# Two network blocks on one core: a weight unit split by full-width instructions, hi products ahead of lo products

## The chip, the cores and the metric

The kernel runs on one core of a Trainium2 chip. The time is the device's time of one execution in microseconds, the median of three runs. The engines are TensorE (PE; its weight loads are PEld), VectorE (DVE), ScalarE (ACT), GpSimd (POOL) and SyncE (SP), which issues the loads.

## What is computed

256 tokens with 1024 channels go through two network blocks in float32. The reference, cut to its frame (the helpers are told in words behind it):

```python
def first_block(x, ...):
    h = rmsnorm(x, norm1_g)
    a_val, a_gate, q, k, v, f_logit, g_a, g_b = jnp.split(h @ w_in, idx, axis=-1)
    ya = conformer_conv(a_val, a_gate, conv_w, conv_b, conv_ln_g, conv_ln_b, w_conv_out)
    ob = forgetting_attention(heads(q), heads(k), heads(v), c)
    yb = ob.transpose(0, 2, 1, 3).reshape(B, S, FOX_W) @ w_fox_out
    x = x + (jax.nn.sigmoid(g_a) * ya + jax.nn.sigmoid(g_b) * yb) @ w_out
    x = x + peer_ffn(rmsnorm(x, norm2_g), peer_wq, peer_k1, peer_k2, peer_u, peer_v)
    return rmsnorm(x, normf_g)

def second_block(x, mem, ...):
    z = rms_norm(x, norm_mix[l]) @ w_in[l]
    ...
    x = x + jnp.sum(gates * proj, axis=2) @ w_out[l]
    up = causal_dwconv(rms_norm(x, norm_ffn[l]) @ w_up[l], ffn_conv_w[l], ffn_conv_b[l])
    gate_h, val_h = jnp.split(up, 2, axis=-1)
    x = x + (jax.nn.gelu(gate_h, approximate=True) * val_h) @ w_down[l]
    return rms_norm(x, final_norm[l])
```

The first block has a causal convolution of 31 taps, an attention with 16 heads and a layer of 16384 experts (two products with 16384 x 1024 weights, and a top-16 choice out of 128 x 128 keys). The second has a recurrent branch, a gated linear attention and an attention over a memory, then a feed-forward layer of width 3072.

## The kernel before

All weights are float32 in DRAM and are used once. They come in *units* of 128 x 1024 (some narrower): `load` (lines 226 to 229) brings a unit into one of three `raw` buffers, and `unit` (231 to 252) splits it exactly into two parts of the type float32r: `hi` is the rounded copy, made by ScalarE (line 240), and `lo` is the rest, `raw - hi`, by VectorE (lines 248, 250) or for a share of the halves by GpSimd (line 244). The split goes by halves of 512 columns. `hi` and `lo` have four tiles of 512 columns each (`WBUFS`), which is two units. A tile is free for a later unit when the last product that reads it is done.

The other operand, the activations with their channels on the partitions, is split in the same way into `xh` and `xl`. A product is the sum of hi·xh, hi·xl and lo·xh.

- `ws` (254 to 265) has the weights as the stationary operand: 24 products of 256 columns for one unit. It goes half by half: eight with hi, four with lo, and again.
- `ts_step` and `ts_part` (267 to 277) have the activations as the stationary operand and the weights moving: 12 products of 512 columns for one unit, which accumulate into four banks `accs[t][n]` (t: half of the tokens, n: half of the unit). For each t the order is xh·hi, xh·lo, xl·hi.
- `ts_tail` (279 to 285) takes the last two units of such a sum together, bank by bank, so that the first tokens' sums end early.

The stages in their order, by the profiled execution: the input norm and the convolution's inputs, w_v, and q, k and the gates with the attention (to some 210 us); the output products of the first block; a norm (near 308); the first product of the experts, with the top-k choice and the scatter of the gates beside it (to some 790); the second product of the experts (ts, to 1144); the second block's norm and branches (to 1462); a norm (near 1464); and the feed-forward.

Several things set the order of the work. A scheduler orders each engine's instructions, and `tc.high_priority` moves a unit's load and split ahead of other work. Each engine then works through its list strictly in that order. Under the convolution, 20 of the 31 taps of a channel tile are VectorE's (`conv_tap`, line 394), each reading what the one before it wrote; the other taps are products by ScalarE (line 400) that GpSimd adds up (line 401). `conv` (423 to 431) queues the taps behind the latest split with `tc.issue_after(last_lo[0])`. In `norm_T` (362 to 375) the residual is added (line 318), squared and summed by ScalarE (319), a reciprocal root taken (324, 325), the rows scaled (370), transposed by TensorE (358) and split with the gain (331 on ScalarE, 332 on VectorE). `behind` makes the subtractions of the next unit wait for the scaling.

Of the kernel before, what the change touches and what calls it, by code (L numbers as in the profile page):

```python
# [19 lines left out]
P = 128  # L20
# [6 lines left out]
WBUFS = 4  # L27
# [20 lines left out]
# columns of the packed per-channel vectors  # L48
# [24 lines left out]
def layout(inp):  # L73
# [37 lines left out]
    # a tile of 128: a head's 96 channels and a third of the last head's  # L111
# [54 lines left out]
def tile_kernel(ctx: ExitStack, tc: tile.TileContext, A: dict, out: bass.AP, tap=None):  # L166
# [54 lines left out]
    pri = [0]  # L221
    last_lo = [None]
    behind = [0, None]  # so many splits wait for that instruction
# [7 lines left out]
    def unit(ap, n):  # L231
        """[128, n] from DRAM -> two halves [128, n/2], each as (hi, lo)"""
        out = []
        with tc.high_priority(offset=pri[0]):
            raw = load(ap, n)
            for c in (0, n // 2):
                hi = stream.tile([P, 512], F32R, name="whi", bufs=WBUFS)
                lo = stream.tile([P, 512], F32R, name="wlo", bufs=WBUFS)
                src, hi, lo = raw[:, c:c + n // 2], hi[:, :n // 2], lo[:, :n // 2]
                act.copy(hi, src)  # L240
                shift[1] += shift[0]
                if shift[1] >= 1:  # a share of them for GpSimd
                    shift[1] -= 1
                    gp.tensor_sub(lo, src, hi.bitcast(F32))  # L244
                elif behind[0] > 0:
                    behind[0] -= 1
                    with tc.issue_after(behind[1]):
                        last_lo[0] = dve.tensor_sub(lo, src, hi.bitcast(F32)).ins
                else:
                    last_lo[0] = dve.tensor_sub(lo, src, hi.bitcast(F32)).ins  # L250
                out.append((hi, lo))
        return out

    def ws(o, ap, width, xt, kc=8):
        """o[n, t] = sum_k w[k, n] x[k, t]"""
# [3 lines left out]
        for i, (hi, lo) in enumerate(w):  # L259
            c = [slice(k * width, (k + 1) * width) for k in range(hk)]  # L260
            for k in range(hk):
                pe.matmul(o, hi[:, c[k]], xh[:, i * hk + k, :], start=(i + k == 0), stop=False)  # L262
                pe.matmul(o, hi[:, c[k]], xl[:, i * hk + k, :], start=False, stop=False)  # L263
            for k in range(hk):
                pe.matmul(o, lo[:, c[k]], xh[:, i * hk + k, :], start=False, stop=(i == 1 and k == hk - 1))  # L265

    def ts_part(accs, w, xh, xl, t, first, last, ns=(0, 1)):
# [5 lines left out]
    def ts_step(accs, ap, width, xh, xl, first, last):  # L273
        """accs[t][n] += x[k, t] w[k, n] for one k; xh, xl: [128, 256]"""
        w = unit(ap, width)
        for t in range(2):
            ts_part(accs, w, xh, xl, t, first, last)
# [1131 lines left out]
```

## Time and profile before

| | |
|---|---|
| median of three runs | 1680.26 us (1679.18, 1680.26, 1681.85) |
| span of the profiled execution | 1679.7 us |
| TensorE busy | 1636.7 us (97%), 11346 products |
| VectorE busy | 1239.0 us (74%) |
| ScalarE busy | 1059.9 us (63%) |
| GpSimd busy | 263.1 us (16%) |
| mean granted clock of TensorE | 0.997 |

The page gives the profiled execution's time as its span, from the first to the last instruction; a timed run also has what lies around it. A share over the whole span mixes stages: under the convolution VectorE has no gaps, in the experts' second product it has many. Products overlap, so that a busy TensorE may still stand still for short times; the distance from one product's start to the next tells more. An instruction's duration is longer than its distance to the next one on the same engine, as the next begins before it has quite ended.

### The profile page before, as it was taken

The page shows a single profiled execution, that of the slowest core. Times are in us where ns is not written, and L with a number is a line of the kernel's source. Part 1 is how long each engine was busy: PE and PEld are TensorE (multiplying, and loading weights), DVE is VectorE, ACT ScalarE, POOL GpSimd, SP SyncE. Part 2 cuts the span into 40 slices and gives each one's busy share as a digit, 9 for nine tenths or more (in the row PEclk, how much of TensorE's full clock was granted, in tenths as well). Part 3 has the DMA queues.
Part 4 walks back from the last instruction along what each step waited for, and adds up shares of the span by engine and source line. Part 5 has one row for each costly group of instructions (what it writes and reads, how often), then busy time and mean ns, then how long its engine had stood idle before and what let it go on. Part 6 is the DMA issues. An engine that isn't in the chain of part 4 may idle for free.

```text
span 1679.7 us, 31312 instructions
## 1 busy us (share of the span) xinstructions
PE 1636.7 (97%) x11346; PEld 1525.6 (91%) x11346; DVE 1239.0 (74%) x2616; ACT 1059.9 (63%) x2337; POOL 263.1 (16%) x255
## 2 busy tenths in 40 slices
PE   7899999999999999999999999999999999999998
PEld 7788999899999999999888888888999999899997
DVE  7999967677989997666656665557765556787777
ACT  7767675555567778776555555556776555566665
POOL 5434200000015444443000000001310000000000
PEclk9999999999999999999999999999999999999999
DMA  5443355555654444445666666666444355565553
GB/s 170 140 151 103 124 154 182 172 176 184 180 180 148 134 139 152 150 142 184 190 192 190 194 188 191 198 191 201 158 136 152 102 183 178 177 201 186 184 184 136
DMA packets 79963, 280.49 MB, mean 167 GB/s; under 512 B 9008, under 2 KB 10304, under 8 KB 79808
## 3 DMA queue, kind: packets, MB, share of 16 engines
q1 hardware_dynamic: 79520, 277.96, 52.6%
q8 instruction: 89, 1.46, 0.4%
q14 instruction: 66, 0.54, 0.1%
q10 hardware_dynamic: 288, 0.52, 0.1%
HBM read 277.40 MB, written 1.05 MB: 166 GB/s over the span
## 4 chain that ended last, share of the span: by engine, by line
PE 84%; DVE 9%; ACT 2%; issue 2%; DMA 1%; POOL 1%; SPq 0%; POOLq 0%; DVEq 0%; ACTq 0%
PE acc L270 30%; PE mm L265 16%; PE mm L262 16%; PE mm L263 16%; DVE wlo L250 3%; PE acc L835 3%; DVE ca L394 2%; ACT whi L240 1%; PE mm L1026 1%; DMA raw<-in_w_mk_dram 0%; PE mm L733 0%; DMA raw<-in_w_conv_in_dram 0%; DVE oh L780 0%; DVE oh L777 0%; POOL cg L401 0%
## 5 line engine op out<-in xcount | busy, mean ns | idle before, releaser
L250 DVE TENSOR_TENSOR wlo<-raw,whi 128x512 fp32r<-128x512 f32 (+2 forms) x987 | 661.0, 691 | 278.3 <-ACT whi L240 272.8
L240 ACT CAST whi<-raw 128x512 fp32r<-128x512 f32 (+1 forms) x1060 | 620.3, 606 | 358.9 <-PE mm L263 220.5
L262 PE MATMUL mm<-xT_hi,whi 128*128 128x256 f32 (+1 forms) x2024 | 514.9, 287 | 3.2 <-ACT sgA L579 1.1
L263 PE MATMUL mm<-xT_lo,whi 128*128 128x256 f32 (+1 forms) x2024 | 507.1, 283 | 0.0
L262 PEld LDWEIGHTS mm<-xT_hi,whi 128*128 128x128 f32 (+1 forms) x2024 | 386.5, 191 | 6.5 <-DVE xT_lo L332 1.9
L263 PEld LDWEIGHTS mm<-xT_lo,whi 128*128 128x128 f32 (+1 forms) x2024 | 387.0, 192 | 1.1
L265 PE MATMUL mm<-xT_hi,wlo 128*128 128x256 f32 (+1 forms) x2024 | 327.6, 284 | 9.7 <-DVE wlo L250 9.5
L265 PEld LDWEIGHTS mm<-xT_hi,wlo 128*128 128x128 f32 (+1 forms) x2024 | 278.8, 191 | 13.6 <-DVE wlo L250 13.1
L270 PE MATMUL acc<-whi,ah 128*128 128x512 f32 x512 | 158.6, 390 | 0.0
L270 PE MATMUL acc<-whi,al 128*128 128x512 f32 x512 | 158.2, 389 | 0.0
L270 PE MATMUL acc<-wlo,ah 128*128 128x512 f32 x512 | 158.2, 389 | 0.0
L244 POOL TENSOR_TENSOR wlo<-raw,whi 128x512 fp32r<-128x512 f32 x69 | 96.7, 1401 | 378.3 <-ACT whi L240 299.3
L325 POOL TENSOR_TENSOR rs<-rs,mhalf 128x1 f32<-128x1 f32 x14 | 10.1, 720 | 784.5 <-DVE rs L324 784.5
L270 PEld LDWEIGHTS acc<-wlo,ah 128*128 128x128 f32 x512 | 96.1, 188 | 20.2 <-DVE wlo L250 0.2
L270 PEld LDWEIGHTS acc<-whi,al 128*128 128x128 f32 x512 | 96.1, 188 | 20.0
L270 PEld LDWEIGHTS acc<-whi,ah 128*128 128x128 f32 x512 | 95.7, 188 | 19.8 <-ACT whi L240 0.2
L299 DVE TENSOR_TENSOR al<-S,ah 128x512 fp32r<-128x512 f32 x64 | 44.2, 692 | 70.0 <-ACT ah L298 70.0
L394 DVE SCALAR_TENSOR_TENSOR ca<-zc,pk,ca 128x256 f32<-128x256 f32 x152 | 91.3, 603 | 1.7
L298 ACT CAST ah<-S 128x512 fp32r<-128x512 f32 x64 | 39.8, 623 | 78.7 <-PE acc L270 78.7
L262 PE MATMUL mm<-h_hi,whi 128*128 128x256 f32 (+1 forms) x344 | 88.1, 288 | 0.0
L263 PE MATMUL mm<-h_lo,whi 128*128 128x256 f32 (+1 forms) x344 | 86.7, 284 | 0.0
L401 POOL TENSOR_TENSOR cg<-cg,cm 128x256 f32<-128x256 f32 x80 | 73.9, 925 | 21.2 <-ACT cg L397 8.3
(436 smaller groups left out, 2414.5 us busy)
## 6 DMA issues: line engine op xcount, KB each, us to landing
raw<-in_u_dram SPq DMA_DIRECT2D x128, 512.0 KB, 3.6
raw<-in_v_dram SPq DMA_DIRECT2D x128, 512.0 KB, 3.6
raw<-in_w_up_dram SPq DMA_DIRECT2D x48, 512.0 KB, 3.7
raw<-in_z_gate_dram SPq DMA_DIRECT2D x24, 512.0 KB, 3.8
raw<-in_w_down_dram SPq DMA_DIRECT2D x24, 512.0 KB, 4.1
raw<-in_w_br_dram SPq DMA_DIRECT2D x24, 384.0 KB, 2.9
raw<-in_w_conv_in_dram SPq DMA_DIRECT2D x16, 512.0 KB, 3.6
raw<-in_w_out_dram SPq DMA_DIRECT2D x16, 512.0 KB, 3.8
```

Of the source, the lines that this page charges most:

```text
L240: act.copy(hi, src)
L244: gp.tensor_sub(lo, src, hi.bitcast(F32))
L250: last_lo[0] = dve.tensor_sub(lo, src, hi.bitcast(F32)).ins
L262: pe.matmul(o, hi[:, c[k]], xh[:, i * hk + k, :], start=(i + k == 0), stop=False)
L263: pe.matmul(o, hi[:, c[k]], xl[:, i * hk + k, :], start=False, stop=False)
L265: pe.matmul(o, lo[:, c[k]], xh[:, i * hk + k, :], start=False, stop=(i == 1 and k == hk - 1))
L270: pe.matmul(accs[t][n], l[:, t * P:(t + 1) * P], w[n][p], start=(first and f), stop=(last and e))
L298: act.copy(hi, src)
L299: dve.tensor_sub(lo, src, hi.bitcast(F32))
L394: dve.scalar_tensor_tensor(ca[:, cb, :], z, w, ca[:, cb, :], op0=OP.mult, op1=OP.add)
L401: gp.tensor_add(cg[cb], cg[cb], m)
L835: pe.matmul(b[:, i, :], o1[:, i, :], o2[:, i, :], start=True, stop=True)
```

## The change

`unit` takes one `hi` and one `lo` tile of 1024 columns, of which there are now two each, so the memory is the same. One copy and one subtraction make them. Where GpSimd has its share, it takes the first half of `lo` and VectorE the rest. `behind` counts units and not halves. In `ws` all 16 hi products of a unit come before its 8 lo products; in `ts_step` all 8 hi products, for both halves of the tokens, come before the 4 lo products. In `ts_part` the order is xh·hi, xl·hi, xh·lo, in the tail too. Which products are formed, and from what, is as before.

```diff
-WBUFS = 4
+WBUFS = 2
...
             raw = load(ap, n)
-            for c in (0, n // 2):
-                hi = stream.tile([P, 512], F32R, name="whi", bufs=WBUFS)
-                lo = stream.tile([P, 512], F32R, name="wlo", bufs=WBUFS)
-                src, hi, lo = raw[:, c:c + n // 2], hi[:, :n // 2], lo[:, :n // 2]
-                act.copy(hi, src)
-                shift[1] += shift[0]
...
+            hi = stream.tile([P, 1024], F32R, name="whi", bufs=WBUFS)
+            lo = stream.tile([P, 1024], F32R, name="wlo", bufs=WBUFS)
+            act.copy(hi[:, :n], raw[:, :n])
+            shift[1] += 2 * shift[0]
+            c = 0
+            if shift[1] >= 1:
+                shift[1] -= 1
+                c = n // 2
+                gp.tensor_sub(lo[:, :c], raw[:, :c], hi[:, :c].bitcast(F32))
+            with tc.issue_after(behind[1]) if behind[0] > 0 else nullcontext():
+                last_lo[0] = dve.tensor_sub(lo[:, c:n], raw[:, c:n], hi[:, c:n].bitcast(F32)).ins
+            behind[0] = max(0, behind[0] - 1)
+        return [(hi[:, c:c + n // 2], lo[:, c:c + n // 2]) for c in (0, n // 2)]
...
-        for i, (hi, lo) in enumerate(w):
-            c = [slice(k * width, (k + 1) * width) for k in range(hk)]
+        c = [slice(k * width, (k + 1) * width) for k in range(hk)]
+        for i, (hi, _) in enumerate(w):
             for k in range(hk):
                 pe.matmul(o, hi[:, c[k]], xh[:, i * hk + k, :], start=(i + k == 0), stop=False)
                 pe.matmul(o, hi[:, c[k]], xl[:, i * hk + k, :], start=False, stop=False)
+        for i, (_, lo) in enumerate(w):
             for k in range(hk):
                 pe.matmul(o, lo[:, c[k]], xh[:, i * hk + k, :], start=False, stop=(i == 1 and k == hk - 1))
...
-        for (l, p, f, e) in ((xh, 0, True, False), (xh, 1, False, False), (xl, 0, False, True)):
+        for (l, p, f, e) in ((xh, 0, True, False), (xl, 0, False, False), (xh, 1, False, True)):
+            if "hl"[p] not in parts:
+                continue
...
-        for t in range(2):
-            ts_part(accs, w, xh, xl, t, first, last)
+        for part in "hl":
+            for t in range(2):
+                ts_part(accs, w, xh, xl, t, first, last, parts=part)
...
-                behind[:] = [2, i.ins]
+                behind[:] = [1, i.ins]
```

How the instructions stand, at two places. VectorE under the convolution's inputs (`wlo` is a lo tile, `ca` the sum of the taps, `zc` their input), before:

```order
L250 TENSOR_TENSOR wlo_657<-raw_654,whi_656 128x512
L394 SCALAR_TENSOR_TENSOR ca_161<-zc_159,pk_74,ca_161 128x256
L250 TENSOR_TENSOR wlo_661<-raw_654,whi_660 128x512
L394 SCALAR_TENSOR_TENSOR ca_161<-zc_159,pk_74,ca_161 128x256 x2
L250 TENSOR_TENSOR wlo_694<-raw_691,whi_693 128x512
L394 SCALAR_TENSOR_TENSOR ca_161<-zc_159,pk_74,ca_161 128x256
L250 TENSOR_TENSOR wlo_698<-raw_691,whi_697 128x512
```

The same place in the changed program:

```order
L245 TENSOR_TENSOR wlo_609<-raw_606,whi_608 128x1024
L393 SCALAR_TENSOR_TENSOR ca_161<-zc_159,pk_74,ca_161 128x256 x3
L245 TENSOR_TENSOR wlo_642<-raw_639,whi_641 128x1024
L442 TENSOR_TENSOR zc_159<-mm_502,sg_602 128x256
L393 SCALAR_TENSOR_TENSOR ca_161<-zc_159,pk_74,ca_161 128x256 x3
```

The three taps of a unit, which the second half's subtraction parted, now follow each other.

ScalarE at the norm ahead of the feed-forward (`hrow0`, `hrow1` are the squares of the two halves of the tokens, `whi` the copies of the next two units), before:

```order
L319 ACTIVATE hrow0_17906,ss_17908<-x0_67 128x512
L240 CAST whi_17979<-raw_17977 128x512
L319 ACTIVATE hrow0_17906,ss_17908<-x0_67 128x512
L240 CAST whi_17983<-raw_17977 128x512
L319 ACTIVATE hrow1_17907,ss_17916<-x1_68 128x512
L240 CAST whi_18018<-raw_18016 128x512
L319 ACTIVATE hrow1_17907,ss_17916<-x1_68 128x512
L240 CAST whi_18022<-raw_18016 128x512
L331 ACTIVATE xT_hi_17928<-mm_17930,gcol_69 128x256
```

The same place in the changed program:

```order
L318 ACTIVATE hrow0_16143,ss_16145<-x0_67 128x512 x2
L237 CAST whi_16216<-raw_16214 128x1024
L318 ACTIVATE hrow1_16144,ss_16153<-x1_68 128x512
L237 CAST whi_16251<-raw_16249 128x1024
L318 ACTIVATE hrow1_16144,ss_16153<-x1_68 128x512
L330 ACTIVATE xT_hi_16165<-mm_16167,gcol_69 128x256
```

Two whole copies stand now before the last two squares, where single halves stood between all of them.

## Rows read from the trace of the kernel before

**Rows 1.** Busy time by stretch: us, then busy us of each engine (instructions), clock, DMA

```profile
24.00:94.00 70.00, 59.78 (x385) 51.45 (x384) 68.43 (x107) 49.55 (x106) 38.16 (x41) 0.98 0.44 137
...
108.00:180.00 72.00, 65.45 (x493) 61.70 (x493) 71.22 (x163) 47.80 (x127) 31.97 (x35) 0.98 0.37 115
...
798.00:1134.00 336.00, 336.00 (x1491) 278.28 (x1490) 201.79 (x326) 178.36 (x328) 0.56 (x1) 1.00 0.61 192
...
1344.00:1428.00 84.00, 84.00 (x704) 84.00 (x703) 51.72 (x97) 47.38 (x90) 0.00 (x0) 1.00 0.55 180
```

**Rows 2.** Waits of TensorE, whole span, then 1134 to 1260: us, times, longest us

```profile
PE mm L265 <- DVE wlo L250: 9.8, 14, 2.1
...
PE acc L270 <- DVE wlo L250: 3.2, 4, 1.2
...
PE mm L265 <- DVE wlo L250: 1.6, 3, 0.7
```

**Rows 3.** Groups by form: xcount, busy us, mean ns; of 24-94, 108-180, 798-1134, whole span

```profile
L250 DVE TENSOR_TENSOR wlo<-raw,whi 128x512 fp32r<-128x512 f32 x36 | 31.5, 892 | 0.7 <-ACT whi L240 0.7
...
L250 DVE TENSOR_TENSOR wlo<-raw,whi 128x512 fp32r<-128x512 f32 x31 | 25.8, 834 | 0.1
...
L250 DVE TENSOR_TENSOR wlo<-raw,whi 128x512 fp32r<-128x512 f32 x246 | 158.7, 686 | 63.3 <-ACT whi L240 63.3
...
L250 DVE TENSOR_TENSOR wlo<-raw,whi 128x384 fp32r<-128x384 f32 x96 | 51.6, 555 | 29.3 <-ACT whi L240 28.6
...
L240 ACT CAST whi<-raw 128x512 fp32r<-128x512 f32 x960 | 572.3, 617 | 322.1 <-PE mm L263 191.8 <-PE acc L270 93.9 <-issue 8.6
...
L240 ACT CAST whi<-raw 128x384 fp32r<-128x384 f32 x96 | 47.0, 511 | 36.5 <-PE mm L263 28.7 <-PE acc L270 5.3 <-DVE s L976 1.2
```

**Rows 4.** VectorE in order of time, GpSimd silent: start us, us, instruction

```profile
112.31 1.00 DVE L394 SCALAR_TENSOR_TENSOR ca<-zc,pk,ca 128x256 f32<-128x256 f32 x2
...
113.22 0.68 DVE L250 TENSOR_TENSOR wlo<-raw,whi 128x512 fp32r<-128x512 f32 x1
...
113.82 0.48 DVE L394 SCALAR_TENSOR_TENSOR ca<-zc,pk,ca 128x256 f32<-128x256 f32 x1
...
114.22 0.68 DVE L250 TENSOR_TENSOR wlo<-raw,whi 128x512 fp32r<-128x512 f32 x1
```

**Rows 5.** VectorE and GpSimd in order of time while both run

```profile
23.50 19.39 POOL L401 TENSOR_TENSOR cg<-cg,cm 128x256 f32<-128x256 f32 x20 [7.19 <-ACT cm L400]
...
30.37 1.23 DVE L250 TENSOR_TENSOR wlo<-raw,whi 128x512 fp32r<-128x512 f32 x1
...
31.52 0.95 DVE L394 SCALAR_TENSOR_TENSOR ca<-zc,pk,ca 128x256 f32<-128x256 f32 x1
```

**Rows 6.** The norm ahead of the feed-forward, four engines in order of time

```profile
1461.83 0.39 PE L270 MATMUL acc<-whi,xT_lo 128*128 128x512 f32 x1
...
1463.05 0.63 ACT L319 ACTIVATE hrow<-x 128x512 f32<-128x512 f32 x1
...
1465.49 0.68 DVE L248 TENSOR_TENSOR wlo<-raw,whi 128x512 fp32r<-128x512 f32 x1
...
1465.73 0.60 PE L358 MATMUL acc<-ident,hrow 128*128 128x128 f32 x4
...
1466.11 1.66 DVE L332 SCALAR_TENSOR_TENSOR xT_lo<-mm,gcol,xT_hi 128x256 fp32r<-128x256 f32 x4
...
1466.65 0.39 PE L262 MATMUL mm<-xT_hi,whi 128*128 128x256 f32 x1 [0.32 <-DVE xT_lo L332]
```

**Rows 7.** The first norm of the program, in order of time

```profile
9.88 1.14 ACT L240 CAST whi<-raw 128x512 fp32r<-128x512 f32 x2 [0.16 <-DMA raw<-in_w_conv_in_dram]
...
10.54 1.06 PE L358 MATMUL acc<-ident,hrow 128*128 128x128 f32 x4
...
11.42 1.66 DVE L332 SCALAR_TENSOR_TENSOR xT_lo<-mm,gcol,xT_hi 128x256 fp32r<-128x256 f32 x4 [0.20 <-ACT xT_hi L331]
```

**Rows 8.** Busy time by stretch, columns as in group 1

```profile
1457.00:1469.00 12.00, 9.73 (x58) 7.85 (x57) 9.53 (x21) 8.71 (x23) 1.12 (x2) 1.00 0.26 86
```

More of the change, by code (lines that the diff above doesn't have):

```diff
@@ L231, in unit @@
     def unit(ap, n):
-        out = []
         with tc.high_priority(offset=pri[0]):
             raw = load(ap, n)
-            for c in (0, n // 2):
-                hi = stream.tile([P, 512], F32R, name="whi", bufs=WBUFS)
-                lo = stream.tile([P, 512], F32R, name="wlo", bufs=WBUFS)
-                src, hi, lo = raw[:, c:c + n // 2], hi[:, :n // 2], lo[:, :n // 2]
-                act.copy(hi, src)
-                shift[1] += shift[0]
[L242 to L252, printed above, removed]
+            hi = stream.tile([P, 1024], F32R, name="whi", bufs=WBUFS)
[11 more added lines that the diff above has]
+        return [(hi[:, c:c + n // 2], lo[:, c:c + n // 2]) for c in (0, n // 2)]
     def ws(o, ap, width, xt, kc=8):
@@ L263, in ws, with ts_part @@
                 pe.matmul(o, hi[:, c[k]], xl[:, i * hk + k, :], start=False, stop=False)
+        for i, (_, lo) in enumerate(w):
             for k in range(hk):
                 pe.matmul(o, lo[:, c[k]], xh[:, i * hk + k, :], start=False, stop=(i == 1 and k == hk - 1))
-    def ts_part(accs, w, xh, xl, t, first, last, ns=(0, 1)):
-        for (l, p, f, e) in ((xh, 0, True, False), (xh, 1, False, False), (xl, 0, False, True)):
+    def ts_part(accs, w, xh, xl, t, first, last, ns=(0, 1), parts="hl"):
+        for (l, p, f, e) in ((xh, 0, True, False), (xl, 0, False, False), (xh, 1, False, True)):
+            if "hl"[p] not in parts:
+                continue
             for n in ns:
```

## The prediction

> **What bounds the kernel now.** I read the busy time by stretch first, because the mean over the span mixes stages with different limits. In 798 to 1134 us (the second product of the experts, all of it ts units) TensorE is busy for 336.00 of 336 us while VectorE is at 202 and ScalarE at 178; in 1344 to 1428 us, among ws units, it is 84.00 of 84 [rows 1]. There TensorE sets the pace by itself: 336/1491 = 0.225 us from one 512-column product to the next, and 84/704 = 0.119 us for 256 columns. The change leaves the number and the form of the products alone, so nothing is to be won in these stretches. It is otherwise in 24 to 94 and 108 to 180 us, under the convolution: VectorE is busy for 68.43 of 70 and 71.22 of 72 us, TensorE for 59.78 and 65.45 [rows 1]. There VectorE sets the pace. Third, the waits: TensorE stands 9.8 us before lo products of ws and 3.2 us before those of ts, with the split's subtraction as the releaser [rows 2]; only 1.6 us of that lie in 1134 to 1260, the head of the second block. The reader is to see that some 13 us of waits are within reach, most of them where VectorE is full anyway, so that moving a wait is not the same as removing it. The rest of the stall is at the norms, where TensorE is idle between two stages.
>
> **The change, step by step.**
>
> *Fixed cost on VectorE.* A subtraction of 512 columns takes 0.60 us from its start to the next one (113.22 to 113.82) [rows 4]. Between 384 and 512 columns the mean grows from 555 to 686 ns [rows 3], 131 ns for 128 columns, so 512 more columns cost 0.52 us: one of 1024 takes 1.13 us where the two took 1.21. That is 0.08 us a unit. The stretches 24 to 94 and 108 to 180 hold 36 and 31 half subtractions [rows 3], 33.5 units: -2.7 us. Ends: 0, and -5.4, were both halves paid at their full 686 ns (1.372 - 1.21 = 0.16 a unit). I take the middle one, since the engine runs without a gap there. [...]
>
> *Taps that now stand side by side.* In the order of instructions a tap followed directly by another tap becomes more frequent, 82 pairs against 50 of 152 taps, because a whole unit's subtraction stands where two halves parted the taps. A tap takes 0.40 us before a subtraction (113.82 to 114.22), two in a row 0.91 (112.31 to 113.22), so 0.51 before another tap of the same tile [rows 4]. 32 x 0.11 = 3.5 us, if all were bare; about half of them run while GpSimd works (38.16 of 70 and 31.97 of 72 us [rows 1]), where a tap waits for GpSimd in any case. I take +1.8 (0 to +3.5). So the two effects on VectorE nearly cancel: -0.9.
>
> *GpSimd's turns.* With GpSimd at its additions (20 in 19.39 us) a subtraction takes 1.15 us (30.37 to 31.52) in place of 0.60 [rows 5]: each GpSimd instruction costs VectorE some 0.55 us. The additions stay as many, so I take 0 (a gain is a rival). The Trainium skill, SBUF — State Buffer, section Who interferes with whom, says that a VectorE instruction with two SBUF inputs and a GpSimd instruction that reads SBUF take a common lock, and the one that comes second waits for the whole of the other. The trace agrees: 0.55 us is paid by an instruction, not by a column. By that rule a longer subtraction also holds GpSimd off for longer; it speaks against the change wherever GpSimd's result is awaited.
>
> *Later need of lo.* In ws the lo products now come after 16 hi products (1.9 us at 0.119) and not after 8. In a stretch in which VectorE is full this only moves the wait. It pays where the lag ends: in w_v (near 88 us) lo is needed after 8 of 12 products and not after 2, so 6 x 0.225 = 1.4 us of work is done ahead of the last wait: -1.4 (0 to -3.2, all ts waits [rows 2]). In 1134 to 1260 the waits sum to 1.6 [rows 2]; a later but longer subtraction ends some of them: -1.0 (0 to -1.6).
>
> *The norms, which lose.* ScalarE's order in front of the transposes was square, copy, square, copy, square, copy, square, copy; now it is two squares, copy, square, copy, square. By the groups a copy takes 617 ns at 512 columns and 511 at 384 [rows 3], 106 ns for 128, hence 1.04 us at 1024. Moreover the first tile that a copy can take is free only when the tail's whole unit has been read, its last hi product being the 20th of 24: four products of 0.225 before the one that starts at 1461.83 [rows 6], so at some 1461.4 with its own 0.39. That copy then ends at 1462.4, the third square at 1463.0, the second copy at 1464.05, and the last square starts there in place of 1463.05 [rows 6]: +1.0 us. Behind it come the reciprocal root, the scaled rows, and on VectorE one subtraction, now 1.13 and not 0.62 us (1465.49 to 1466.11), ahead of the first lo part of the normalized rows, which TensorE waits for (1466.65) [rows 6]: +0.5. TensorE is idle there and nothing covers it. The norm ahead of the experts has the same order: 2 x 1.5 = +3.0. Ends: 2 x 0.5 = +1.0, and 2 x 2.0 = +4.0 with half a microsecond more for a copy that starts late.
>
> *The start.* Three half subtractions precede the first normalized lo part, which starts at 11.42 [rows 7]. Now there are two whole ones, and the second waits for a copy of 1.04 us from 9.88: 9.88 + 1.04 + 1.13 = 12.05. +0.6 (0 to +0.9).
>
> *Costed at nothing.* ScalarE saves some 0.19 us a unit, but is at 178 of 336 us where TensorE is full [rows 1] and waits there for TensorE. The first of two hi buffers is free after two thirds of a unit, and a copy and a subtraction (2.2 us) fit into the unit after it (12 x 0.225 = 2.7); were that cover gone, each of the units would lose some 0.5 us. The input's buffer is held at most 0.5 us longer in ws. Under the top-k stage the half that GpSimd takes stays one of two.
>
> **Sum.** -2.7 + 1.8 + 0 - 1.4 - 1.0 + 3.0 + 0.6 = +0.3 us. The profiled span is 1679.7 us and the median of the three timed runs 1680.26, 0.6 more, which I leave around the span: 1679.7 + 0.3 + 0.6 = 1680.6 us. A difference below 0.2%, 3.4 us, is no change here, being what a measurement of this kernel can tell.
>
> **The rivals.** *Fewer turns for GpSimd (faster).* Half of the 33.5 units fall into GpSimd's bursts, and each has one subtraction less that can be held up. If those turns are not taken back later but fall where VectorE has time, 17 x 0.55 = 9 us go: 1671.6. For it: VectorE is full there, with GpSimd at 38.16 and 31.97 us [rows 1]. Against: 80 additions remain, and each finds an instruction to hold up. Chance 0.12. *Waits that vanish (faster).* If the 13.0 us of waits for lo [rows 2] are unevenness and not a full VectorE, the eight further hi products cover two thirds of them: -8.7, with the norms' losses already in, less the 2.4 counted above: 1674.3. Chance 0.13. *The clock falls at the longer norms (slower).* TensorE's granted clock is 1.00 in 1457 to 1469 [rows 8], with idle stretches of a microsecond, and 0.98 in the two VectorE-bound stretches [rows 1], so it does fall in mid-kernel. If 1.5 us more of idling bring the lower level (1.2 GHz), 16 transposes cost what they do at the start, 1.06 us for four [rows 7] against 0.60 [rows 6], +1.8, and some ten products at twice 0.119 +1.2: 2 x 3.0 = 6 us: 1686.6. It decides from the point at which the clock of that stretch reads below 1. Chance 0.22. The Trainium skill, TensorE: Matmul & The Clock Gate, Part 1, says that an idle array drops to the half clock; no row here shows it at a norm.
>
> **How the numbers follow.** My forecast has 0.53, with an own range of 1676 to 1685 by the ends above (not all of them fall together), which puts 0.04 of it below 0.2% and 0.08 above. Faster: 0.12 + 0.13 + 0.04 = 0.29; slower: 0.22 + 0.08 = 0.30; within 0.2%: 0.41. The range of 8 in 10 takes in the clock's case and the nearer of the gains: 1672 to 1687.
>
> **What would show it.** VectorE: subtractions of 1024 columns at 1.13 us start to start, taps at 0.51 in threes. TensorE: waits for lo below 13 us, but idle time before VectorE's rows at the norms up by some 1.5 us each. The stretches with TensorE full: 0.225 and 0.119 us a product as before (if those move, the sum is wrong at its base: 2 ns on each of the 1491 products of 798 to 1134 would be 3 us there alone). VectorE well below full in 24 to 180 us would speak for the gains.

## The result, and the profile after

The changed kernel takes 1697.42 us (median of four runs, 1695.86 to 1699.22) against 1680.50 us for the kernel before (also four, 1679.18 to 1681.85), a ratio of 1.0100 with a 95% interval of 1.0088 to 1.0112. The prediction was 1680.6 us, no change, with a range up to 1687. It was wrong by 16.8 us. The profiled execution has a span of 1695.3 us.

**Where the 15.6 us of span went.** Both programs issue 11346 products in the same order of units, so the n-th product of one stands at the same place of the work, within a unit, as the n-th of the other. I follow ten of them through both traces, and the end. A product's lateness is its start in the changed kernel minus its start before.

| start before, us | what lies ahead of it | lateness, us | step |
|---|---|---|---|
| 0 (first product) | loads of the input | +0.82 | +0.8 |
| 24 | first norm, first units | +1.17 | +0.4 |
| 300 | first block | -2.49 | -3.7 |
| 340 | norm ahead of the experts | +0.36 | +2.9 |
| 504 | queries, first experts | +0.36 | 0 |
| 574 | experts beside the second top-k's maxima | +7.60 | **+7.2** |
| 642 | experts beside its one-hot rows | +12.13 | **+4.5** |
| 1134 | rest of the experts | +12.13 | 0 |
| 1300 | second block's branches | +13.74 | +1.6 |
| 1500 | norm ahead of the feed-forward | +15.17 | +1.4 |
| end | feed-forward | +15.63 | +0.5 |

Three quarters lie in one stage that the prediction did not cost. I call its two parts A (504 to 574 us before, 596 products) and B (574 to 642, 547 products).

The stretches of [rows 1], in the changed kernel (us, then busy us of PE, PEld, DVE, ACT, POOL with instructions, clock, DMA):

```profile
24.00:94.00 70.00, 60.89 (x405) 53.00 (x403) 68.06 (x91) 49.99 (x91) 43.02 (x41) 1.00 0.46 139
...
108.00:180.00 72.00, 65.67 (x512) 63.77 (x510) 68.89 (x148) 47.92 (x114) 34.62 (x35) 0.98 0.39 117
...
798.00:1134.00 336.00, 336.00 (x1525) 279.67 (x1524) 195.26 (x207) 167.15 (x208) 2.39 (x2) 1.00 0.64 194
...
1344.00:1428.00 84.00, 84.00 (x696) 83.34 (x695) 46.12 (x66) 42.14 (x62) 1.01 (x1) 1.00 0.56 171
```

Under the convolution VectorE is full as before from 24 to 94 us, and 405 products fit into 70 us where 385 did; from 108 to 180 us it is no longer quite full (68.89 of 72 us against 71.22). Where TensorE is full, nothing changed (a window of fixed times holds other units, so its counts of products differ a little; the lateness of 12.13 us at 642 and at 1134 says it better).

The waits of TensorE, whole span, answering [rows 2]:

```profile
PE mm L257 <- ACT whi L237: 7.6, 9, 1.5
PE mm L261 <- DVE wlo L245: 5.9, 7, 1.2
...
PE mm L794 <- DVE S L790: 2.8, 1, 2.8
PE acc L268 <- DVE wlo L245: 2.4, 4, 0.9
```

The waits for lo fell from 13.0 to 8.3 us (5.9 + 2.4), as the order of products makes one expect. Waits for hi, 7.6 us, have taken their place; before, the same wait for hi came to 0.4 us.

The groups, answering [rows 3] (the first is of 24 to 94 us, the second of 798 to 1134):

```profile
L245 DVE TENSOR_TENSOR wlo<-raw,whi 128x1024 fp32r<-128x1024 f32 x20 | 29.2, 1460 | 2.2 <-ACT whi L237 2.2
...
L245 DVE TENSOR_TENSOR wlo<-raw,whi 128x1024 fp32r<-128x1024 f32 x122 | 149.4, 1225 | 138.2 <-ACT whi L237 138.2
```

One whole subtraction lasts 1.23 us where VectorE is not disturbed, against 2 x 0.686. Under the convolution it is 1.46 against 2 x 0.892: which fits a whole one being held up once beside GpSimd where two halves are held up twice.

**The stage that lost.** Parts A and B, first of the kernel before, columns as above:

```profile
504.07:574.00 69.93, 69.93 (x596) 69.93 (x595) 68.94 (x246) 52.85 (x149) 32.70 (x28) 1.00 0.46 140
574.00:642.48 68.48, 66.67 (x547) 64.78 (x547) 66.09 (x143) 51.48 (x150) 33.04 (x28) 1.00 0.45 142
```

The same products in the changed kernel:

```profile
504.44:581.60 77.16, 72.79 (x596) 70.78 (x595) 75.75 (x246) 49.45 (x131) 34.12 (x29) 1.00 0.44 130
581.60:654.61 73.01, 67.79 (x547) 66.20 (x547) 68.72 (x142) 52.53 (x139) 35.72 (x29) 0.98 0.46 138
```

In A VectorE is as full after as before, and has 6.8 us more to be full with (75.75 against 68.94). Which group holds most of them? The subtractions of A, before:

```profile
L250 DVE TENSOR_TENSOR wlo<-raw,whi 128x512 fp32r<-128x512 f32 x25 | 17.0, 684 | 0.0
...
L244 POOL TENSOR_TENSOR wlo<-raw,whi 128x512 fp32r<-128x512 f32 x12 | 15.9, 1325 | 22.6 <-ACT whi L240 15.6 <-PE acc L835 3.9 <-DVE o L808 2.0
```

and after:

```profile
L245 DVE TENSOR_TENSOR wlo<-raw,whi 128x512 fp32r<-128x512 f32 x13 | 13.7, 1057 | 0.0
L245 DVE TENSOR_TENSOR wlo<-raw,whi 128x1024 fp32r<-128x1024 f32 x6 | 7.2, 1208 | 0.0
...
L243 POOL TENSOR_TENSOR wlo<-raw,whi 128x512 fp32r<-128x512 f32 x13 | 17.3, 1331 | 36.8 <-ACT whi L237 24.4 <-DVE o L820 6.7 <-DVE sc L738 5.5
```

The half that is left to VectorE when GpSimd takes the other one now lasts 1057 ns in place of 684, on average over thirteen (ten of them above 750 ns; before, one of 25); the whole subtractions are undisturbed at 1208. Together that is 3.9 of the 6.8 us (20.9 against 17.0); another 1.5 us are rows of the scatter that fall into A or beside a turn (`o`, 512 columns, 12.4 against 10.9). VectorE and GpSimd in order of time show why. A GpSimd turn before (start us, us):

```profile
527.68 0.28 DVE L739 MAX8 v<-S 128x8 f32<-128x128 f32 x1
527.73 1.28 POOL L244 TENSOR_TENSOR wlo<-raw,whi 128x512 fp32r<-128x512 f32 x1 [2.54 <-ACT whi L240]
527.89 0.27 DVE L743 MAX8 v<-S 128x8 f32<-128x128 f32 x1
...
528.14 0.28 DVE L740 FIND_INDEX8 i<-v,S 128x8 uint32<-128x128 f32 x1
...
528.40 0.28 DVE L745 FIND_INDEX8 i<-v,S 128x8 uint32<-128x128 f32 x1
```

and one after:

```profile
543.30 1.03 ACT L237 CAST whi<-raw 128x1024 fp32r<-128x1024 f32 x1
...
544.41 1.30 POOL L243 TENSOR_TENSOR wlo<-raw,whi 128x512 fp32r<-128x512 f32 x1 [1.67 <-ACT whi L237]
...
544.76 0.28 DVE L741 MATCH_REPLACE8 S<-v,S 128x128 f32<-128x128 f32 x1
544.95 1.31 DVE L245 TENSOR_TENSOR wlo<-raw,whi 128x512 fp32r<-128x512 f32 x1
```

Before, VectorE goes through maxima and indices at their usual 0.28 us while GpSimd subtracts. After, one copy (543.30, 1.03 us) releases both halves, so VectorE's own half comes up 0.54 us after GpSimd's, and it ends only at 546.26, 0.55 us behind the end of GpSimd's at 545.71 (1.31 us and not 0.67): it waits GpSimd's out and then needs nearly its own time. This is the *pair theory*: the two halves of a unit, released together, run into each other. Its rivals: the *ScalarE theory* (the whole copy stands behind the scatter's copies in ScalarE's list and TensorE waits for hi), and the *order theory* (hi first holds the buffers of lo too long).

In B the picture is another one. The subtractions (L250, L245) and the one-hot rows (`oh`), before:

```profile
L250 DVE TENSOR_TENSOR wlo<-raw,whi 128x512 fp32r<-128x512 f32 x23 | 16.2, 720 | 1.6 <-ACT whi L240 1.5
L780 DVE TENSOR_TENSOR oh<-oh,S 128x256 f32<-128x256 f32 x16 | 11.3, 707 | 0.3
...
L777 DVE TENSOR_TENSOR oh<-S,iotaf 128x256 f32<-128x256 f32 x16 | 10.3, 647 | 0.0
```

and after:

```profile
L245 DVE TENSOR_TENSOR wlo<-raw,whi 128x512 fp32r<-128x512 f32 x14 | 16.5, 1180 | 2.0 <-ACT whi L237 2.0
...
L776 DVE TENSOR_TENSOR oh<-S,iotaf 128x256 f32<-128x256 f32 x16 | 8.8, 555 | 0.0
...
L779 DVE TENSOR_TENSOR oh<-oh,S 128x256 f32<-128x256 f32 x16 | 7.0, 440 | 0.4
...
L245 DVE TENSOR_TENSOR wlo<-raw,whi 128x1024 fp32r<-128x1024 f32 x5 | 6.1, 1215 | 0.0
```

The subtractions take 6.4 us more (22.6 against 16.2), but the one-hot rows, which the turns held up before, take 5.8 less (15.8 against 21.6; without a share, in e4, 13.2). What TensorE loses in B is mostly one wait and the clock behind it, shown further below.

### The profile page after: what moved, and what is told of

Same layout as the page of the kernel before. It is cut to its first block, busy times and chain, and to the rows that moved or that the text cites. A ratio compares the mean times of both kernels' runs of the same rounds, so it can differ in the third digit from the quotient of the medians.

```text
span 1695.3 us, 29624 instructions
## 1 busy us (share of the span) xinstructions
PE 1640.2 (97%) x11346; PEld 1529.2 (90%) x11346; DVE 1208.7 (71%) x2155; ACT 991.7 (58%) x1807; POOL 295.5 (17%) x255
## 3 DMA queue, kind: packets, MB, share of 16 engines
q8 instruction: 89, 1.46, 0.4%
## 4 chain that ended last, share of the span: by engine, by line
PE 77%; DVE 14%; ACT 3%; issue 2%; POOL 2%; DMA 1%; SPq 0%; POOLq 0%; ACTq 0%; DVEq 0%
PE acc L268 29%; PE mm L257 14%; PE mm L258 14%; PE mm L261 14%; DVE wlo L245 5%; PE acc L834 2%; ACT whi L237 2%; DVE ca L393 2%; POOL cg L400 2%; DVE o L807 1%; PE mm L1025 1%; DVE S L826 1%; DVE o L820 0%; PE mm L732 0%; PE mm L1227 0%
## 5 line engine op out<-in xcount | busy, mean ns | idle before, releaser
L245 DVE TENSOR_TENSOR wlo<-raw,whi 128x1024 fp32r<-128x1024 f32 (+2 forms) x530 | 618.6, 1168 | 393.6 <-ACT whi L237 373.2
L237 ACT CAST whi<-raw 128x1024 fp32r<-128x1024 f32 (+1 forms) x530 | 543.2, 1026 | 512.1 <-PE mm L258 244.3
L257 PE MATMUL mm<-xT_hi,whi 128*128 128x256 f32 (+1 forms) x2024 | 506.2, 288 | 13.2 <-ACT whi L237 7.6
L258 PE MATMUL mm<-xT_lo,whi 128*128 128x256 f32 (+1 forms) x2024 | 498.2, 284 | 0.0
L261 PE MATMUL mm<-xT_hi,wlo 128*128 128x256 f32 (+1 forms) x2024 | 286.5, 284 | 6.2 <-DVE wlo L245 5.9
L261 PEld LDWEIGHTS mm<-xT_hi,wlo 128*128 128x128 f32 (+1 forms) x2024 | 261.5, 192 | 8.6 <-DVE wlo L245 8.4
L243 POOL TENSOR_TENSOR wlo<-raw,whi 128x512 fp32r<-128x512 f32 x69 | 110.9, 1608 | 392.7 <-ACT whi L237 353.3
L268 PE MATMUL acc<-wlo,ah 128*128 128x512 f32 x512 | 137.8, 389 | 0.0
L813 POOL TENSOR_SCALAR o<-iotaf,eT 128x128 f32<-128x128 f32 x64 | 74.0, 1157 | 21.2 <-PE acc L834 13.9
L834 PE MATMUL acc<-o,o 128*128 128x128 f32 x512 | 68.6, 277 | 0.4 <-DVE o L807 0.2
```

Source lines behind the costliest of these rows:

```text
L237: act.copy(hi[:, :n], raw[:, :n])
L243: gp.tensor_sub(lo[:, :c], raw[:, :c], hi[:, :c].bitcast(F32))
L245: last_lo[0] = dve.tensor_sub(lo[:, c:n], raw[:, c:n], hi[:, c:n].bitcast(F32)).ins
L268: pe.matmul(accs[t][n], l[:, t * P:(t + 1) * P], w[n][p], start=(first and f), stop=(last and e))
L813: gp.tensor_scalar(o2[:, i, :], iotaf, eT[:, 1, t:t + 1], eT[:, 2, t:t + 1], op0=OP.is_equal, op1=OP.mult)
L834: pe.matmul(b[:, i, :], o1[:, i, :], o2[:, i, :], start=True, stop=True)
```

## The experiments

Times are medians, ratios against the kernel before run on the same chip. A and B are the times of those same products in each trace.

| run | us | ratio (95%) | A, us | B, us |
|---|---|---|---|---|
| before | 1680.50 | | 69.93 | 68.48 |
| changed | 1697.42 | 1.0100 (1.0088 to 1.0112) | 77.16 | 73.01 |
| e1 split only | 1694.71 | 1.0082 (1.0065 to 1.0099) | 75.98 | 70.73 |
| e2 order only | 1690.51 | 1.0058 (1.0041 to 1.0075) | 77.97 | 69.86 |
| e3 changed, no share | 1683.21 | 1.0016 (1.0007 to 1.0026) | 71.07 | 64.24 |
| e4 before, no share | 1679.94 | 0.9997 (0.9988 to 1.0007) | 70.92 | 64.75 |
| e5 GpSimd takes whole units | 1686.83 | 1.0047 (1.0032 to 1.0063) | 71.31 | 68.59 |
| e6 half the share | 1690.30 | 1.0065 (1.0050 to 1.0080) | 74.10 | 68.84 |
| e7 wide in first block | 1684.70 | 1.0027 (1.0016 to 1.0038) | 70.86 | 64.74 |
| e8 norms in halves, no share | 1680.88 | 1.0009 (1.0000 to 1.0018) | 71.06 | 64.37 |
| e9 as e7, buffers earlier | 1679.61 | 0.9993 (0.9984 to 1.0002) | 70.87 | 64.77 |
| e10 order only, no share | 1682.40 | 1.0003 (0.9994 to 1.0013) | 71.95 | 64.18 |
| e11 half copies at turns | 1694.35 | 1.0089 (1.0074 to 1.0105) | 74.50 | 72.67 |
| e12 changed, share in A alone | 1690.38 | 1.0062 (1.0045 to 1.0079) | 77.17 | 65.74 |
| e13 before, share in A alone | 1680.41 | 0.9996 (0.9987 to 1.0006) | 69.92 | 65.93 |

### The two parts of the change alone (e1, e2)

e1 is the changed kernel with the products in the order of the kernel before (`ts_part` and `ts_step` likewise):

```diff
-        for i, (hi, _) in enumerate(w):
+        for i, (hi, lo) in enumerate(w):
...
-        for i, (_, lo) in enumerate(w):
             for k in range(hk):
                 pe.matmul(o, lo[:, c[k]], xh[:, i * hk + k, :], start=False, stop=(i == 1 and k == hk - 1))
```

> Whole-width split with the order of products of the kernel before (per half: hi, then lo). Collision theory (in 504 to 654 us GpSimd's half and VectorE's half of one unit are released by the same ScalarE copy, run on each other, and VectorE's 512-column subtraction grows from a mean of 702 to 1120 ns, 27 x 0.42 = 11 us): the loss of that stage stays, 512-column subtractions there again at about 1.1 us, and lo, now needed after 8 of 16 hi products, brings more waits for lo: 1697 to 1706 us. Order theory (the loss comes from hi first, both lo parts last, two coarse buffers): most of the loss goes, 1680 to 1686. ScalarE theory (the whole copy stands behind the scatter's copy in ScalarE's list, and TensorE waits for the whole hi): as the collision theory in the total, but 512-column subtractions of VectorE stay near 0.70 us and the waits for hi near 5 us.

e2 is the kernel before with the new `ws`, `ts_part` and `ts_step`, its `unit` untouched.

> Half-width split of the kernel before with the new order of products (hi first). Collision theory: no loss in the expert stage, VectorE's 512-column subtractions there at a mean of 0.70 us; the waits for lo of ws shrink by 1 to 4 us; nothing at the norms: 1675 to 1681 us. Order theory: 1690 to 1698. ScalarE theory: as the collision theory, 1676 to 1682, since the copies are halves again.

e1 measured 1694.71 us. It lies 2.3 us below the range of the pair theory (there called collision theory), but its 512-column subtractions are held up as that theory wants (1025 ns on average over A and B, expected about 1.1 us); in A, where lo is needed after 8 products, TensorE now waits 4.4 us for lo. The order theory's 1680 to 1686 is refuted for the split alone. e2 measured 1690.51 and so met the order theory's number, not mine. But its subtractions in A show the same hold-up:

```profile
L250 DVE TENSOR_TENSOR wlo<-raw,whi 128x512 fp32r<-128x512 f32 x25 | 21.1, 863 | 0.0
```

863 ns against 684, and single pairs look like those of the changed kernel:

```profile
520.57 1.28 POOL L244 TENSOR_TENSOR wlo<-raw,whi 128x512 fp32r<-128x512 f32 x1 [2.05 <-ACT whi L240]
520.68 1.72 DVE L250 TENSOR_TENSOR wlo<-raw,whi 128x512 fp32r<-128x512 f32 x1
```

So each part alone can bring VectorE's and GpSimd's subtraction together (in e2's A, five of 25 last above 1.3 us). For the order the likely reason, argued and not shown, is that the first half's lo tile is now free only after the unit's 20th product and not its 12th, close to the second's after the 24th. Whether the order costs by itself, e10 decides.

### The share taken away (e3, e4, e10)

```diff
-LO_U = 0.35
+LO_U = 0
```

in the changed kernel, in the kernel before, and in e2.

> The changed kernel with no share of the subtractions for GpSimd in the expert stage. All 38 units of that stretch are subtracted whole on VectorE at 1.21 us: 27 x (1.21 - 1.12) = 2.4 us more VectorE work than now, less what the one-hot rows give back with GpSimd idle. Collision theory: about the same time as the changed kernel, 1694 to 1702, and within 4 us of its sibling below (kernel before without the share), because the difference of the two lies in the collisions alone. ScalarE theory: still 8 to 12 us above that sibling, waits for hi near 5 us.

> The kernel before with no share of the subtractions for GpSimd in the expert stage: some 26 half subtractions more on a full VectorE, 26 x 0.6 = 15 us at most: 1688 to 1697 us. Collision theory: the difference of the run above minus this one is what lies outside this stage and a little less (+4 to 0 us, from the norms +4, the second block +2, the convolution -4 and the fixed cost -3). ScalarE theory: run above minus this one is +8 to +14 us.

> Half-width split, new order of products, no share for GpSimd in the expert stage. Pair theory (with hi first the lo buffers of a unit come free close together, at its 20th and 24th product in place of the 12th and 24th, so its two subtractions stand next to each other and GpSimd's holds up VectorE's): without the share nothing is held up, the +9.4 us of that stage go to about -3: 1676 to 1680 us. If the order itself holds up the split (lo buffers freed late, whoever subtracts): 1686 to 1691 us.

The difference of e3 and e4 is 3.3 us, where the pair theory had 0 to 4 and the ScalarE theory 8 to 14: the ScalarE theory falls. The level was missed: I had expected VectorE to pay for the work it takes back, 1694 to 1702 and 1688 to 1697 us. Both came out far lower. With the share gone, the changed kernel's A and B are:

```profile
506.02:577.09 71.07, 70.42 (x596) 70.06 (x595) 70.69 (x239) 51.22 (x133) 15.44 (x16) 1.00 0.45 144
577.09:641.33 64.24, 64.24 (x548) 64.16 (x547) 62.16 (x143) 49.93 (x131) 17.98 (x15) 1.00 0.47 150
```

TensorE is full or nearly (70.42 of 71.07, 64.24 of 64.24), and VectorE has less to do in all than with help (70.69 + 62.16 = 132.85 us against 144.47): what GpSimd took over came back as time held up. In the kernel before the share is worth nothing either (e4 0.9997): its two parts take 135.67 us without it and 138.41 with it. e10 at 1682.40 lies 2.4 above my upper end but 3.6 below the other theory's lower end; A and B fall by 11.7 us against e2, to what e4 has within half a microsecond in sum. The order costs there only through the share.

### How the turns are taken (e5, e6, e11)

e5 gives GpSimd whole units:

```diff
-            shift[1] += 2 * shift[0]
-            c = 0
+            shift[1] += shift[0]
             if shift[1] >= 1:
                 shift[1] -= 1
-                c = n // 2
-                gp.tensor_sub(lo[:, :c], raw[:, :c], hi[:, :c].bitcast(F32))
+                gp.tensor_sub(lo[:, :n], raw[:, :n], hi[:, :n].bitcast(F32))
+            else:
...
```

e6 halves the share (`LO_U = 0.175`). e11 copies hi in two halves where GpSimd has a turn:

```diff
-            act.copy(hi[:, :n], raw[:, :n])
...
                 c = n // 2
+                act.copy(hi[:, :c], raw[:, :c])
+            act.copy(hi[:, c:n], raw[:, c:n])
+            if c:
                 gp.tensor_sub(lo[:, :c], raw[:, :c], hi[:, :c].bitcast(F32))
```

> The changed kernel, but where GpSimd takes a turn it subtracts a whole unit (35 of 100 units), and VectorE none of that unit; the share of columns is the same as in the changed kernel (one half of 70 in 100). Pair theory (the loss of the expert stage arises where the two halves of one unit are released together, one on GpSimd and one on VectorE, and run on each other): no pairs are left, VectorE's subtractions there go back to about 1.21 us for 1024 columns, and most of the 14 us between the changed kernel and the one without the share returns: 1683 to 1689 us. Share theory (each us that GpSimd subtracts costs VectorE and the products the same, paired or not): no better than the changed kernel; a whole lo of some 2.7 us also comes later than the 1.9 us of hi products in front of it: 1692 to 1699 us.

> The changed kernel with half the share for GpSimd (0.175 in place of 0.35), so some 13 turns in the expert stage and not 27. If each turn costs the same (pair and share theory alike): midway between 1683.2 (no turns) and 1697.4 (27 turns), 1689 to 1692 us. If the loss is a threshold (VectorE's list overfull only beyond some point): 1683 to 1686, or still 1695 and more.

> The changed kernel, but for units with a GpSimd turn hi is copied in two halves, GpSimd's first, so GpSimd's subtraction can start 0.5 us ahead of VectorE's of the same unit; the share is unchanged. Pair theory: VectorE's half now reaches GpSimd's turn (1.28 us) later, about 0.5 us less of waiting in each of 27 turns, at most 12 us: 1685 to 1692 us, and VectorE's 512-column subtractions of the expert stage at a mean of 0.7 to 0.9 us against 1.12. If VectorE is held up for the whole of GpSimd's turn wherever it falls: 1693 to 1698 us, and 1.0 us or more.

e5 measured 1686.83, inside the pair theory's range: the same columns on GpSimd, but no partner, give back 10.6 us, and A is within 0.3 us of the run without a share. In B it is not: 68.59 us against 64.24, so there a turn costs without a partner too. e6 at 1690.30 lies midway: no threshold, each turn costs. e5 and e6 also settle whether it is the number of turns or the columns moved: both have 13 turns in A and B, e6 with half the columns, and yet e6's A is 74.10 us and e5's 71.31. In A it is the pair. e11 at 1694.35 returned 3 us and lies where the other case had it, though its subtractions (957 ns over A and B) lie between the two. Its subtractions, first in A, then in B, tell why:

```profile
L247 DVE TENSOR_TENSOR wlo<-raw,whi 128x512 fp32r<-128x512 f32 x13 | 10.3, 796 | 0.3 <-POOL o L815 0.2
...
L247 DVE TENSOR_TENSOR wlo<-raw,whi 128x512 fp32r<-128x512 f32 x14 | 15.5, 1107 | 2.2 <-ACT whi L243 2.2
```

In A the head start works (796 ns, A shorter by 2.7 us). In B it does not: there other things that GpSimd holds up stand around it (the one-hot rows of `oh<-oh,S` last 682 ns, in the changed kernel 440). So A and B had to be told apart.

### The share in part A alone (e12, e13)

```diff
                 e = scr(96, 3)
+                hot[0] = t == 1
...
-                shift[0] = LO_U if live[0] is False or live[1] is False or n[1] else 0
+                shift[0] = LO_U if (live[0] is False or live[1] is False or n[1]) and not hot[0] else 0
```

in the changed kernel and in the kernel before.

> The changed kernel with GpSimd's share only up to the end of the second top-k's maxima (some 504 to 574 us), none beside its one-hot rows. Pair theory (in that stretch VectorE's half of the same unit is what follows GpSimd's turn, and is held up): the loss of that stretch, 5 to 6 us at 567 us in the changed kernel, stays, and the stage behind it goes as without the share: 1687 to 1690 us. If holding up costs only beside the one-hot rows, where VectorE has no other kind of work: 1683 to 1685 us, as without any share.

> The kernel before with the same restriction: the turns up to 574 us alone. There its turns lie beside maxima, indices and replacements, which its trace shows at their usual length (0.28 us) while GpSimd subtracts. Pair theory: these turns cost nothing, 1679 to 1681 us, and 6 us or more below the run above. If a turn costs the same in both kernels: 1683 us and more, or both runs as without the share.

Measured: 1690.38 and 1680.41 us, 10.0 apart, as the pair theory had it (the first by 0.4 over its range). A and B of e12, then of e13:

```profile
504.40:581.57 77.17, 72.78 (x596) 70.78 (x595) 75.76 (x246) 49.44 (x131) 34.11 (x29) 1.00 0.42 130
581.57:647.31 65.74, 64.59 (x548) 64.27 (x547) 63.05 (x140) 51.11 (x134) 14.78 (x15) 1.00 0.49 152
```

```profile
501.53:571.45 69.92, 69.92 (x596) 69.92 (x595) 68.92 (x246) 52.81 (x150) 32.70 (x28) 1.00 0.45 140
571.45:637.38 65.93, 64.38 (x547) 64.15 (x547) 63.35 (x157) 52.66 (x153) 19.75 (x15) 1.00 0.49 151
```

With the same share in A, the kernel before has TensorE full for 69.92 of 69.92 us, and the changed one needs 77.17. Against the runs without a share (70.92 and 71.07) the turns in A gain 1.0 us before and lose 6.1 after. In B they cost in both: 3.7 before (68.48 - 64.75), 8.8 after (73.01 - 64.24); against e13 and e12, which differ in B's turns alone, 2.6 and 7.3. So the pair theory is shown for A. For B it is shown that the turns cost, and more in the changed kernel, but not that it is the pairs that cost.

### The norms, and a search for the better of both (e8, e7, e9)

e8 is e3 with copies and subtractions in halves for the two units behind a norm:

```diff
+            fine = behind[0] > 0
+            for a, b in ((0, n // 2), (n // 2, n)) if fine else ((0, n),):
+                act.copy(hi[:, a:b], raw[:, a:b])
...
+            for a, b in ((0, n // 2), (n // 2, n)) if fine else ((c, n),):
+                with tc.issue_after(behind[1]) if fine else nullcontext():
+                    last_lo[0] = dve.tensor_sub(lo[:, a:b], raw[:, a:b], hi[:, a:b].bitcast(F32)).ins
...
-                behind[:] = [1, i.ins]
+                behind[:] = [2, i.ins]
```

> The changed kernel without the share for GpSimd in the expert stage, and with the two units behind each of the two norms copied and subtracted in halves (in the whole tiles). If the norms' +2.9 and +1.5 us come from the copies' length in ScalarE's order and the whole subtraction ahead of the rows, most of that returns: 1679.5 to 1681.5 us against 1683.2 without the halves. If it comes from the coarser buffers (the tail's whole unit must be read before the next copy starts): 1682 to 1684 us.

1680.88 us, as expected if the copies' length and the whole subtraction make the norms' cost. The norm ahead of the experts in the changed kernel, TensorE and VectorE in order of time ([rows 6] has the same steps at the other norm, with a half subtraction and a last wait of 0.32):

```profile
307.88 0.65 PE L357 MATMUL mm<-ident,hrow 128*128 128x128 f32 x4 [1.54 <-DVE hrow L369]
308.13 1.22 DVE L245 TENSOR_TENSOR wlo<-raw,whi 128x1024 fp32r<-128x1024 f32 x1
...
309.80 0.58 PE L257 MATMUL mm<-xT_hi,whi 128*128 128x256 f32 x1 [0.83 <-DVE xT_lo L331]
```

and in e8:

```profile
308.04 0.66 PE L360 MATMUL mm<-ident,hrow 128*128 128x128 f32 x4 [1.19 <-DVE hrow L372]
...
309.45 0.39 PE L260 MATMUL mm<-xT_hi,whi 128*128 128x256 f32 x1 [0.32 <-DVE xT_lo L334]
```

The second wait, 0.83 us behind a whole subtraction, is 0.32 again with halves. The first goes from 1.54 to 1.19, not all the way to what the kernel before has there:

```profile
309.41 0.66 PE L358 MATMUL mm<-ident,hrow 128*128 128x128 f32 x4 [0.68 <-DVE hrow L370]
```

The half microsecond that is left is likely that of the whole tile, free only when all of the tail's unit has been read; no run shows that by itself.

e7 uses the changed unit in the first block alone and the unit of the kernel before behind it, without a share; e9 is e7 with the two lines that set the buffers aside moved up:

```diff
+    w1 = tc.tile_pool(name="w1", bufs=2)
+    wpool[0] = w1.__enter__()
     with tc.tile_pool(name="p0", bufs=1) as p0:
...
     pri[0] = PRI
-    w1 = tc.tile_pool(name="w1", bufs=2)
-    wpool[0] = w1.__enter__()
```

> The changed unit and order in the first block alone (up to 304 us), the unit and order of the kernel before behind it, and no share for GpSimd in the expert stage. If the parts add: -2.5 us from the first block, +1 at the norm behind it, and the 0.2 us that the missing share gives by itself: 1677 to 1680 us. If the gain of the first block is only time moved ahead of the norm, or the switch of buffers costs at the norm: 1680 to 1682 us.

> As the run with the changed unit in the first block alone, but its buffers are set aside before the first norm, not behind it. If that run lost its 4.7 us between 0 and 24 us because the first units waited for the memory of the first norm's rows (+5.9 us at 24 us, the changed kernel has +1.2), those come back: 1678 to 1681 us by 1684.7 - 4.7, and 1676 to 1678 if the second block too goes as in the kernel before. If the start is lost to something else: 1683 to 1686 us.

e7 missed at 1684.70: its product at 24 us came 5.9 us late, in e9 1.2 us, as in the changed kernel. The place of the buffers was nearly all of it (4.7 us at that product, of 5.1 between the two medians). e9 at 1679.61 has the lowest median of the study, but its interval (0.9984 to 1.0002) takes in no change, as do those of e4 and e13. No version was measurably faster than the kernel before.

## Why the prediction was wrong

**The step that failed** is in the paragraph *Costed at nothing*: "Under the top-k stage the half that GpSimd takes stays one of two." The number of turns did stay the same (12 and 13 in A). What changed is what VectorE has in hand when a turn begins. It now has its own half of the unit, which waits GpSimd's out: ten of the 13 in A are held up, and the 13 last 1057 ns on average in place of 684. This stage cost 11.8 us (7.2 + 4.5, before rounding) and nothing in the sum stood for it. Two things were in my own text. *GpSimd's turns* priced a hold-up at 0.55 us from [rows 5], and then counted only the convolution's additions. And it said that the rule of the lock "speaks against the change wherever GpSimd's result is awaited": I looked at who waits for GpSimd, not at VectorE's own next instruction. The Trainium skill (SBUF — State Buffer, Who interferes with whom) has both: an instruction of VectorE with two SBUF inputs contends with a GpSimd instruction that reads SBUF, and one with a single SBUF input, outside VectorE's two-port modes, does not. The rows agree: 1.31 us for the subtraction, which reads two tiles, beside 0.28 for MAX8, which reads one. FIND_INDEX8 and MATCH_REPLACE8, whose rows name two, keep their 0.28 as well.

How VectorE's time becomes TensorE's, in A: VectorE's subtractions take 20.9 us (13.7 + 7.2) where they took 17.0, though GpSimd's help was the same. The rest of its list comes later, and ScalarE, in order, waits for the scatter's rows (first before, then after):

```profile
ACT S L829 <- DVE S L827: 10.1, 11, 2.3
```

```profile
ACT S L828 <- DVE S L826: 24.7, 15, 4.3
```

Behind those copies stand the copies of hi, and TensorE waits for hi (3.2 us in A, before none). That much of the ScalarE theory holds, as a consequence. In B, 2.8 us are one wait of the transposes (L794) for a result of VectorE's, and behind it the granted clock reads 0.61 for 4 us:

```profile
648.00:652.00 4.00, 3.96 (x22) 3.97 (x23) 3.61 (x9) 3.85 (x14) 2.56 (x2) 0.61 0.53 139
```

There are 22 products in these 4 us, where the kernel before has 36 in 660 to 664 us at clock 1.00, so some 1.5 us more. The wait and the clock together are about the 4.5 us of B. The same wait stands in e6 and e11 (2.7 us each) and, with 1.6, in e5, whose turns have no partner; e12, without turns in B, has 1.1, the kernel before and e3 none.

There is one more difference that I had not counted: before, a turn spared VectorE a whole instruction of 0.67 us; now it makes one of 1.21 into one of 0.67, 0.13 us less for each of the 27 turns.

**The other steps.**

- *Fixed cost, taps, later need of lo in the first block*: -2.7 + 1.8 - 1.4 = -2.3, with the gain at GpSimd's turns a rival. Measured from 24 to 300 us: -3.7, and -2.8 to -5.0 in the profiles of e3, e5, e6, e8, e9, e11 and e12, which have the whole unit there too. Undivided units under the convolution do help, somewhat more than I said; the group's mean of 1460 ns against 2 x 892 shows that being held up once and not twice is part of it, the rival that I gave 0.12. The kernel before has a scatter of its own there, e4 -0.15 and e13 -2.25 with the same unit, so the size stays uncertain by some 2 us. A part of it may be the clock, which I had not counted: in the kernel before it reads 0.57 in 88 to 92 and in 177 to 181 us, in the changed kernel 1.00 in both and 0.60 in 152 to 156, one fall less. The size of the fixed cost holds: a whole subtraction takes 1.14 us from its start to the next instruction's (308.13 to 309.27 at the norm), predicted 1.13.
- *The start*: +0.6 predicted, +0.4 measured from the first product to the one at 24 us. That the first product itself is 0.8 us late is no effect of the change: e13 has 0.0, e4 +0.9.
- *The norms*: +1.5 each, by +1.0 for the copies' order and +0.5 for the whole subtraction. Measured at the first: TensorE's two waits grew by 0.86 (0.68 to 1.54) and 0.51 (0.32 to 0.83), together 1.4; at the second the lateness grew by 1.4. The mechanism and the size hold, and e8 shows both. At the first norm 1.5 us came on top: the third rival, the lower clock, in one of its two places.

```profile
310.00:314.00 4.00, 4.00 (x22) 4.00 (x23) 3.62 (x8) 1.27 (x4) 0.00 (x0) 0.60 0.40 131
```

22 products in 4 us, where e8 has 35 at clock 1.00. I had priced the lower clock at 3.0 us a norm, falling at both; it fell at one and cost 1.5 (2.9 of lateness less the 1.4 of waits). In the changed kernel and its variants e3, e5, e6, e11 and e12 a norm cost 1.4 us where the clock stayed up and 1.9 to 3.2 where it fell. The longer norm is not needed for a fall: e13, whose norm ahead of the feed-forward is that of the kernel before, has one there and comes out of that norm 0.9 us later (columns as above):

```profile
1462.00:1466.00 4.00, 4.00 (x25) 4.00 (x24) 3.92 (x10) 3.29 (x9) 0.00 (x0) 0.63 0.01 4
```

- *Second block*: -1.0 predicted, +1.6 measured. The waits for lo did shrink, but the branch waits for its weights (L1025) for 1.9 us, and the clock reads 0.83 from 1240 to 1250 us. Kernels whose code there is that of the kernel before came out between -0.5 (e4) and +2.7 (e9) in the same stretch, so I can't put this on the change.
- *Steady stretches at zero*: right, 0.00 from 642 to 1134 and from 1300 to 1440.
- *Waits that vanish* (0.13): the waits for lo fell by 4.7 of 13.0 us, not by two thirds, and VectorE stayed full from 24 to 94 us and nearly so from 108 to 180.

**What stays open.** Without the share the changed kernel is still 3.3 us above the kernel without it (e3, e4), about what the norms cost; e8 takes 2.3 of them back. e2's mean of 863 ns against 1057 is not less time held up, since it is that of 25 subtractions: they take 21.1 us in e2's A, 20.9 in the changed kernel's and 17.0 before. Why e2 then loses 8.0 us there and the changed kernel 7.2 was not traced further. Nor was it tested what puts VectorE late at the transposes' wait in B.

## What to carry to other kernels

When one instruction releases work on two engines that can hold each other up, the two tend to start together: in A ten of 13 halves were held up so, and one of 25 before, when the same work was released by two instructions half a unit apart and lay beside things that did not mind. So, of a merged or moved producer, ask what each consumer's engine will have next in its list, and try the offloaded share at zero before tuning anything around it: here it was worth nothing before the change and cost 14 us after it. And look for the engine's other work that a turn holds up, which in B cost time without any pair.

## What the runs showed of the hardware that I had not expected

- A VectorE subtraction of 512 columns (two SBUF inputs) that comes up while GpSimd subtracts ends 0.55 us behind it (544.95 + 1.31 against 544.41 + 1.30; in e2 520.68 + 1.72 against 520.57 + 1.28), so that it lasts up to 1.7 us in place of 0.67; MAX8, FIND_INDEX8 and MATCH_REPLACE8 of 128 columns run beside it at 0.28 us, unchanged.
- Help can be negative: with GpSimd's 27 half subtractions VectorE was busy for 144.5 us over A and B, without them, doing all itself, for 132.9.
- The two norms of the changed kernel have the same waits on TensorE (1.54 and 0.83 us at each), and the granted clock was 0.60 in the 4 us behind the first and 1.00 behind the second.
